# A hybrid decoder layer on one core: residual rows parked in device memory, six more raw weight buffers, and four seven-product pairs in nine of the gate/up blocks

## The chip, the core and the metric

The kernel runs on one core of a Trainium2 chip. The metric is the time of one execution on the device in microseconds. The kernel before takes 1085.96 us (median of three runs, 1085.82 to 1085.98). The profile is of one execution, recorded by the hardware.

## The reference

One decoder layer over 256 tokens with model width 2048 and a feed-forward width of 5632, all in float32:

```python
def reference(x, ln1_w, w_in, conv_w, ..., w_out, ln2_w, w_ffn_gate, w_ffn_up, w_ffn_down, final_norm_w):
    h = x
    for l in range(DEPTH):
        u = rmsnorm(h, ln1_w[l])
        proj = jnp.einsum('bsd,de->bse', u, w_in[l])
        lru_x, lru_g, q, k, v, ret_g = jnp.split(proj, SPLITS, axis=-1)
        ...
        y = jnp.concatenate([y_lru, y_ret], axis=-1)
        h = h + jnp.einsum('bse,ed->bsd', y, w_out[l])
        u = rmsnorm(h, ln2_w[l])
        ff = jax.nn.silu(jnp.einsum('bsd,df->bsf', u, w_ffn_gate[l])) * jnp.einsum('bsd,df->bsf', u, w_ffn_up[l])
        h = h + jnp.einsum('bsf,fd->bsd', ff, w_ffn_down[l])
    return rmsnorm(h, final_norm_w)
```

The change touches the output projection (`w_out`), the gate and up products of the feed-forward part, and what of the down product and the final norm hangs on them. `h`, the residual row, is needed at `w_out`, then for `u`, and then only at the down product.

## The kernel before

**A product.** TensorE (PE) multiplies in a reduced float32 format. Each float32 operand is split into a high part (a cast) and a low part (operand less high part), and `three` (L670 to L672) adds three matmuls: high by high, low weight by high left, high weight by low left. The left operands (tokens) are split once and kept. The weights, 235 MB, come past once: SyncE (SP) loads 512 KB at a time into a raw buffer (pool `raw`, six of 128x1024), ScalarE (ACT) casts it into `wh` (L112), VectorE (DVE) subtracts it into `wl` (L113); the pool `split` has four buffers each of `wh` and `wl`. `load` is called three loads ahead of the step that uses them (`AHEAD = 3`).

**Blocks.** From the output projection on, the program is a row of blocks: index 0 and 1 are `w_out`, 2 to 12 the eleven gate/up blocks (each 512 columns of gate and up), then the down product. A block has four accumulators (`c11`, `c12`, `c21`, `c22`: two token tiles by two halves of the columns) and eight quads of weights. A quad is 2x2 tiles b11, b12, b22, b21 in two loads, and it is multiplied in one of two ways:

- plain (`p`, `Block.plain`): eight products, 24 matmuls, two full splits.
- summed, a seven-product pair: DVE adds the quad's tiles into t1 to t4 (`Quad.add`, L648, four 128x512 adds), which are split too. Four products with b11, t1, t2 and t3 are added into the accumulators one block ahead (`s`, `Block.share`, 12 matmuls, loaded by `Shared`); three with b21, b22 and t4 follow in the block itself (`d`, `Block.direct`, 9 matmuls), for which `Direct` loads half of the weights again. That is seven products, 21 matmuls.

`SUMMED[i]` lists the summed quads of block i, `STEPS[i]` the order of its steps; its `s` steps belong to block i+1. After the last `s` of a block `share` combines the accumulators: two copies by ACT (L782, L785) and four operations on DVE (L783 to L787), and the next product that goes into `c12` has to wait for the second copy.

**Between blocks.** A gate/up block ends in `post`: ACT's Silu (L842) and DVE's multiplication (L844); then PE transposes (L833) and ACT copies the result into `ff` (L835). `Left` splits it and builds its sums for the down product (L551 to L554 on DVE). The output projection ends in `out_post`: DVE adds the residual rows `htok` (eight tiles of 128x512, pool `resid`, L585) and ACT squares them for the norm (L586).

**Order.** Each engine runs its instructions in the order that was fixed when the program was built: a scheduler takes the steps in the order of `program`, simulates the engines, and moves an instruction ahead of others where it could start earlier. An engine waits at its first instruction that is not ready. A cast into `wh` waits for the last matmul that reads the buffer's former content, a `wl` waits for the cast.

Of the kernel before, what the change touches and what calls it, by code (L numbers as in the profile page):

```python
# [31 lines left out]
SUMMED = ((), (4, 5), (2, 3)) + ((1, 2, 3), (0, 1, 2, 3)) * 4 + ((1, 2, 3), (1, 2, 3))  # L32
# [3 lines left out]
STEPS = ("pppspppspp", "ppspdpsdpp", "pdpsdpspspp") + ("pspsdpsdpsdp", "psdpsdpsddp") * 4 + ("psdpsdpsdpp", "psdpsdpsdpp")  # L36
# [8 lines left out]
def tile_hymba_layer(ctx: ExitStack, tc: tile.TileContext, A: dict, out: bass.AP):  # L45
# [5 lines left out]
    xpool = ctx.enter_context(tc.tile_pool(name="resid", bufs=8))  # L51
    rpool = ctx.enter_context(tc.tile_pool(name="raw", bufs=6))
    wpool = ctx.enter_context(tc.tile_pool(name="split", bufs=4))
    early = ctx.enter_context(ExitStack())
    epool = early.enter_context(tc.tile_pool(name="conv", bufs=2))
    tpool = early.enter_context(tc.tile_pool(name="tmp", bufs=6))
    late = []
# [12 lines left out]
    def res_tile(name, dt=F32):  # L70
        return xpool.tile([P, 512], dt, tag="xh", name=nm(name))
# [43 lines left out]
    class Unit:  # L115
# [8 lines left out]
        def load(self, j):  # L124
            raw = rpool.tile([P, 1024], F32, tag="raw", name=nm("raw"))
            h = wpool.tile([P, 1024], F32R, tag="wh", name=nm("wh"))
            l = wpool.tile([P, 1024], F32R, tag="wl", name=nm("wl"))
            n = 1024 // self.pieces
            for p in range(self.pieces):
                o = p * n  # L130
                nc.sync.dma_start(out=raw[:, o : o + n], in_=self.src[:, j * 1024 + o : j * 1024 + o + n])
                if self.before:
                    self.before(j * self.pieces + p)
            for p in range(self.pieces):
                o = p * n
                split(h[:, o : o + n], l[:, o : o + n], raw[:, o : o + n])
                if self.after:
                    self.after(j * self.pieces + p)
            self.h.append(h)
            self.l.append(l)  # L140
# [426 lines left out]

    def out_post(d):
# [13 lines left out]
        def post(c, ps):  # L582
            cb, t = 2 * d + int(c[2]) - 1, int(c[1]) - 1
            h = htok[cb, t]
            v.tensor_tensor(out=h, in0=ps, in1=h, op=ALU.add)  # L585
            act.activation(out=act_tile("junk"), in_=h, func=AF.Square, accum_out=sq2[:, t, cb : cb + 1])  # L586
            if t:
                turns.extend(lambda p=p: turn(p) for p in (2 * cb, 2 * cb + 1))
            if (cb, t) == (3, 1):
                v.tensor_reduce(out=v2, in_=sq2, axis=mybir.AxisListType.X, op=ALU.add)  # L590
                rsqrt_small(r2_tok, v2, 1.0 / D, 2)
# [12 lines left out]
    class Quad:  # L604
# [21 lines left out]
        def load(self, half):  # L626
            r = rpool.tile([P, 1024], F32, tag="raw", name=nm("raw"))
# [95 lines left out]
    class Shared(Quad):  # L723
# [4 lines left out]
        def load(self, half):  # L728
            r = rpool.tile([P, 1024], F32, tag="raw", name=nm("raw"))
# [17 lines left out]
    class Direct(Quad):  # L747
# [8 lines left out]
        def load(self, half):  # L756
            r = rpool.tile([P, 1024], F32, tag="raw", name=nm("raw"))
            nc.sync.dma_start(out=r, in_=self.src[:, 1024:2048])
            self.cut(("b22", "b21"), r)
            self.parts["t4"] = self.shared.parts["t4"]  # L760
# [97 lines left out]
    def load_fw():  # L858
        for c in range(4):
            fw[c] = late_tile("fw")  # L860
            nc.sync.dma_start(out=fw[c], in_=A["final_norm_w"][c * 512 : c * 512 + 512].partition_broadcast(P))
# [203 lines left out]
    def swap():  # L1065

        early.close()
        late.append(ctx.enter_context(tc.tile_pool(name="late", bufs=4)))

# [6 lines left out]
    for b, after in zip(blocks, blocks[1:] + [down]):  # L1076
        if b.index == 2:
            program.append(([], swap))
        b.put(after)
        if b.index == NB:  # L1080
            program.append(([], load_fw))
# [120 lines left out]
```

## Time and profile before

| | before |
|---|---|
| median of the runs | 1085.96 us |
| span of the profiled execution | 1084.4 us |
| gate/up blocks 3 to 12 end at | 476.3, 515.4, 560.4, 599.5, 644.5, 683.6, 728.6, 767.7, 811.0, 852.6 us |
| ACT CAST 128x1024 in the stage 432.3 to 852.6 us | 161 times, mean 1051 ns |
| DVE wl 128x1024 there | 160 times, mean 1218 ns |
| DVE adds L648 there | 136, mean 690 ns |
| mean DMA rate of the program | 220 GB/s |

The profiled execution has no time of its own but its span; the median lies 1.6 us above it. In the views, a row of the timeline gives start, length, engine, line, operation and the tiles out<-in; "x3" are instructions of one form run together, and a bracket at the end is the idle time before it and what ended it. Operations overlap a little at their ends, so start to start is the better measure of what an instruction occupies: a full split on DVE is written as 1218 ns and the next one starts 1.14 us after it. In the waits, "ACT wh L112 <- PE c L672" reads: ACT's cast into `wh` waited for a matmul.

### The profile page before, as it was taken

What the parts mean: (1) busy time and instruction counts of PE and PEld (TensorE: products, weight loads), DVE (VectorE), ACT (ScalarE), POOL (GpSimd) and SP (SyncE); (2) the same over time, 40 slices, a digit from 0 to 9 for tenths busy, and PEclk for the clock granted to TensorE, in tenths of its full rate; (3) what the DMA queues carried; (4) which work ended last, traced back from release to release, by engine and by line L of the source; (5) the groups of instructions that cost most, each with busy time, mean ns of one, the idle gap of its engine ahead of it and who ended that gap; (6) DMA issues with size and microseconds to landing.
All of it is one profiled execution on the core that took longest, in us unless ns stands there. A gap on an engine that the chain in (4) does not pass through costs nothing.

```text
span 1084.4 us, 14584 instructions
## 1 busy us (share of the span) xinstructions
PE 1074.2 (99%) x5101; PEld 899.5 (83%) x5101; DVE 953.5 (88%) x1371; ACT 660.9 (61%) x935; POOL 51.0 (5%) x61
## 2 busy tenths in 40 slices
PE   9999999999999999999999999999999999999997
PEld 7888888888888788888888888888888888888885
DVE  7789799988878889888998998999899899898986
ACT  7666644468746676565566566556556666655563
POOL 0612230000000000000000000000000000000001
PEclk9999999999999999999999999999999999999999
DMA  9964474444565567577677677686675756465652
GB/s 330 333 211 168 160 252 173 174 175 171 181 230 205 184 228 275 198 248 266 220 245 261 220 264 235 233 289 214 233 271 194 265 181 213 171 214 199 212 209 85
DMA packets 69274, 238.32 MB, mean 220 GB/s; under 512 B 7888, under 2 KB 8272, under 8 KB 69200
## 3 DMA queue, kind: packets, MB, share of 16 engines
q1 hardware_dynamic: 68400, 235.29, 62.7%
q0 software_dynamic: 512, 1.57, 0.4%
q8 instruction: 40, 0.66, 0.2%
q10 hardware_dynamic: 288, 0.52, 0.1%
q14 instruction: 34, 0.28, 0.1%
HBM read 235.26 MB, written 2.10 MB: 219 GB/s over the span
## 4 chain that ended last, share of the span: by engine, by line
PE 97%; DVE 1%; issue 1%; DMA 0%; ACT 0%; POOL 0%; SPq 0%; POOLq 0%; ACTq 0%
PE c L670 22%; PE c L672 22%; PE c L671 22%; PE fm L184 11%; PE fm L186 5%; PE tm L164 3%; PE tm L165 3%; PE tm L166 3%; PE p L672 1%; PE p L671 1%; PE p L670 1%; PE ft L833 1%; DMA raw<-in_w_v 0%; PE ht L576 0%; PE sc L482 0%
## 5 line engine op out<-in xcount | busy, mean ns | idle before, releaser
L112 ACT CAST wh<-raw 128x1024 fp32r<-128x1024 f32 (+1 forms) x490 | 460.9, 965 | 362.6 <-PE c L672 132.5
L113 DVE TENSOR_TENSOR wl<-raw,wh 128x1024 fp32r<-128x1024 f32 (+1 forms) x490 | 538.2, 1122 | 91.2 <-ACT wh L112 88.4
L671 PE MATMUL c<-wl,ah 128*128 128x512 f32 x850 | 331.0, 390 | 0.0
L672 PE MATMUL c<-wh,al 128*128 128x512 f32 x850 | 330.4, 389 | 0.0
L670 PE MATMUL c<-wh,ah 128*128 128x512 f32 x850 | 275.0, 391 | 0.2 <-ACT wh L112 0.2
L670 PEld LDWEIGHTS c<-wh,ah 128*128 128x128 f32 x850 | 159.4, 188 | 33.4 <-ACT wh L112 1.1
L672 PEld LDWEIGHTS c<-wh,al 128*128 128x128 f32 x850 | 159.6, 188 | 33.0
L671 PEld LDWEIGHTS c<-wl,ah 128*128 128x128 f32 x850 | 159.6, 188 | 32.7
L184 PE MATMUL fm<-u,wh 128*128 128x512 f32 x512 | 161.3, 396 | 0.0
L186 PEld LDWEIGHTS fm<-u,wl 128*128 128x128 f32 x512 | 96.0, 188 | 22.5
L186 PE MATMUL fm<-u,wl 128*128 128x256 f32 x512 | 101.1, 278 | 0.0
L184 PEld LDWEIGHTS fm<-u,wh 128*128 128x128 f32 x512 | 78.4, 189 | 0.3
L648 DVE TENSOR_TENSOR raw<-raw,raw 128x512 f32<-128x512 f32 x106 | 73.1, 690 | 2.8
L648 DVE TENSOR_TENSOR raw<-raw 128x512 f32<-128x512 f32 x106 | 72.7, 689 | 2.4
L671 PE MATMUL c<-wl,sh 128*128 128x512 f32 x176 | 68.5, 389 | 0.0
L672 PE MATMUL c<-wh,sl 128*128 128x512 f32 x176 | 68.0, 389 | 0.0
L670 PE MATMUL c<-wh,sh 128*128 128x512 f32 x176 | 60.4, 394 | 0.3 <-ACT sh L112 0.3
L165 PE MATMUL tm<-wl,u 128*128 128x512 f32 x128 | 48.8, 394 | 0.0
L166 PE MATMUL tm<-wh,u 128*128 128x512 f32 x128 | 48.7, 390 | 0.0
L164 PE MATMUL tm<-wh,u 128*128 128x512 f32 x128 | 47.3, 398 | 0.8 <-ACT u L288 0.8
L954 POOL TENSOR_TENSOR htok<-htok,fw 128x512 f32<-128x512 f32 x2 | 2.5, 1273 | 895.9 <-ACT junk L947 895.9
L670 PEld LDWEIGHTS c<-wh,sh 128*128 128x128 f32 x176 | 33.1, 188 | 7.3 <-ACT sh L112 0.7
(245 smaller groups left out, 1034.9 us busy)
## 6 DMA issues: line engine op xcount, KB each, us to landing
raw<-in_w_gu SPq DMA_DIRECT2D x212, 512.0 KB, 5.5
raw<-in_w_down SPq DMA_DIRECT2D x91, 512.0 KB, 4.3
raw<-in_w_out SPq DMA_DIRECT2D x34, 512.0 KB, 3.7
raw<-in_w_lx SPq DMA_DIRECT2D x16, 512.0 KB, 6.3
raw<-in_w_k SPq DMA_DIRECT2D x16, 512.0 KB, 3.5
raw<-in_w_q SPq DMA_DIRECT2D x16, 512.0 KB, 4.0
raw<-in_w_rg SPq DMA_DIRECT2D x16, 512.0 KB, 3.4
raw<-in_w_lg SPq DMA_DIRECT2D x16, 512.0 KB, 3.4
```

What stands on the lines that cost most here:

```text
L112: act.copy(out=dst_h, in_=src)
L113: v.tensor_tensor(out=dst_l, in0=src, in1=dst_h.bitcast(F32), op=ALU.subtract)
L164: pe.matmul(ps, ah, wh, start=first, stop=False)
L165: pe.matmul(ps, ah, wl, start=False, stop=False)
L166: pe.matmul(ps, al, wh, start=False, stop=last)
L184: pe.matmul(ps, wh, hl, start=n + i == 0, stop=False)
L186: pe.matmul(ps[:, :S], wl, hl[:, :S], start=False, stop=n + i == len(order) - 1)
L648: v.tensor_tensor(out=dst, in0=a, in1=b, op=ALU.add)
L670: pe.matmul(p, ah, bh, start=first, stop=False, skip_group_check=onto)
L671: pe.matmul(p, ah, bl, start=False, stop=False, skip_group_check=onto)
L672: pe.matmul(p, al, bh, start=False, stop=last, skip_group_check=onto)
L833: pe.transpose(pt[:, o : o + P], g[:, (2 * b + c) * P : (2 * b + c) * P + P], ident)
```

## The change

Three things change together.

- The residual rows are written to device memory as soon as they are made (eight stores issued by ACT in `out_post`), their pool and two others are closed ahead of block 3, and after the last block they are read back by eight DMAs on GpSimd's (POOL's) queue. The four loads of the final norm's weights go from SP to POOL and move behind block 12.
- In the space the pool `raw2` of six raw buffers is opened; loads go in turn to the old and the new pool from block 3 until ahead of block 12.
- Blocks 4 to 12 have four summed quads each; before, blocks 4, 6, 8 and 10 had four and 5, 7, 9, 11 and 12 had three. The step strings follow.

```diff
-SUMMED = ((), (4, 5), (2, 3)) + ((1, 2, 3), (0, 1, 2, 3)) * 4 + ((1, 2, 3), (1, 2, 3))
+SUMMED = ((), (4, 5), (2, 3), (1, 2, 3)) + ((0, 1, 2, 3),) * 9
 SUMMED_OUT, SUMMED_FFN = (4, 5), (0, 1, 2, 3)
 PLAIN = ((4, 5, 6, 7, 0, 1, 2, 3),) * 2 + (tuple(range(8)),) * 11
-STEPS = ("pppspppspp", "ppspdpsdpp", "pdpsdpspspp") + ("pspsdpsdpsdp", "psdpsdpsddp") * 4 + ("psdpsdpsdpp", "psdpsdpsdpp")
+STEPS = ("pppspppspp", "ppspdpsdpp", "pdpsdpspspp", "pspsdpsdpsdp") + ("psdpsdpsdpsd"[:-1]+"dp"[:0],)*0 + ("psdpsdsdpsdp",) * 8 + ("psdpsddpsdp",)
 EARLY_DOWN = (0, 1, 2)
...
     apool = ctx.enter_context(tc.tile_pool(name="acts", bufs=60))
-    xpool = ctx.enter_context(tc.tile_pool(name="resid", bufs=8))
     rpool = ctx.enter_context(tc.tile_pool(name="raw", bufs=6))
...
     early = ctx.enter_context(ExitStack())
+    xpool = early.enter_context(tc.tile_pool(name="resid", bufs=8))
     epool = early.enter_context(tc.tile_pool(name="conv", bufs=2))
     tpool = early.enter_context(tc.tile_pool(name="tmp", bufs=6))
-    late = []
+    late, resid, more, turn_of = [], [xpool], [], [0]
+    extra = ExitStack()
     pmm = ctx.enter_context(tc.tile_pool(name="pmm", bufs=4, space=PSUM))
...
     def res_tile(name, dt=F32):
-        return xpool.tile([P, 512], dt, tag="xh", name=nm(name))
+        return resid[0].tile([P, 512], dt, tag="xh", name=nm(name))
+    def raw_tile():
+        turn_of[0] += 1
+        pool_ = more[0] if more and turn_of[0] % 2 else rpool
+        return pool_.tile([P, 1024], F32, tag="raw", name=nm("raw"))
     def late_tile(name, dt=F32):
...
         def load(self, j):
-            raw = rpool.tile([P, 1024], F32, tag="raw", name=nm("raw"))
+            raw = raw_tile()
             h = wpool.tile([P, 1024], F32R, tag="wh", name=nm("wh"))
...
     turns = []
+    kept = nc.dram_tensor("kept_rows", (4, 2, P, 512), F32, kind="Internal").ap()
     def out_post(d):
...
             act.activation(out=act_tile("junk"), in_=h, func=AF.Square, accum_out=sq2[:, t, cb : cb + 1])
+            act.dma_start(out=kept[cb, t], in_=h)
             if t:
...
         def load(self, half):
-            r = rpool.tile([P, 1024], F32, tag="raw", name=nm("raw"))
+            r = raw_tile()
             nc.sync.dma_start(out=r, in_=self.src[:, half * 1024 : half * 1024 + 1024])
...
         def load(self, half):
-            r = rpool.tile([P, 1024], F32, tag="raw", name=nm("raw"))
+            r = raw_tile()
             nc.sync.dma_start(out=r, in_=self.src[:, half * 1024 : half * 1024 + 1024])
...
         def load(self, half):
-            r = rpool.tile([P, 1024], F32, tag="raw", name=nm("raw"))
+            r = raw_tile()
             nc.sync.dma_start(out=r, in_=self.src[:, 1024:2048])
...
             fw[c] = late_tile("fw")
-            nc.sync.dma_start(out=fw[c], in_=A["final_norm_w"][c * 512 : c * 512 + 512].partition_broadcast(P))
+            pool.dma_start(out=fw[c], in_=A["final_norm_w"][c * 512 : c * 512 + 512].partition_broadcast(P))
     ssq = cpool.tile([P, 2, 5], F32, name="ssq")
...
         early.close()
+        more.append(extra.enter_context(tc.tile_pool(name="raw2", bufs=6)))
+    def stop_more():
+        more.clear()
+    def swap_back():
+        extra.close()
         late.append(ctx.enter_context(tc.tile_pool(name="late", bufs=4)))
+        resid[0] = ctx.enter_context(tc.tile_pool(name="resid2", bufs=8))
+        for key in [(cb, t) for cb in range(4) for t in range(2)]:
+            htok[key] = res_tile("htok")
+            pool.dma_start(out=htok[key], in_=kept[key])
+        load_fw()
     blocks = [Block(d, lambda i, d=d: A["w_out"][8 * d + i], y, out_post(d), STEPS[d], SUMMED[d]) for d in range(2)]
...
     for b, after in zip(blocks, blocks[1:] + [down]):
-        if b.index == 2:
+        if b.index == 3:
             program.append(([], swap))
+        if b.index == NB + 1:
+            program.append(([], stop_more))
         b.put(after)
-        if b.index == NB:
-            program.append(([], load_fw))
+    program.append(([], swap_back))
     for d in range(2):
```

The line numbers of the changed kernel are six to nine higher (L113 is L119, L648 is L657, L670 to L672 are L679 to L681, L785 is L794). Counted over the whole program, PE has 15 matmuls fewer, DVE 35 instructions more (20 adds and 15 half splits), ACT 15 casts and 8 DMA issues more, SP one issue more (five weight loads more, four loads of the norm's weights fewer), POOL 12 DMAs more.

First place, DVE in a gate/up block. Before, between one shared step and the next there is a plain quad. The rows begin with the t1/t3 split of a shared quad (`wl_1184`); `wl_1189` is the split of a direct step, `wl_1181` and `t4l_1186` take t2 and t4, `wl_1192` and `wl_1195` are the two halves of a plain quad, `wl_1198` takes b11 of the next shared quad and `wl_1201` its t1/t3:

```order
L113 TENSOR_TENSOR wl_1184_5712<-raw_1179_5688,wh_1183_5711 128x1024
L113 TENSOR_TENSOR wl_1189_5722<-raw_1187_5719,wh_1188_5721 128x1024
L113 TENSOR_TENSOR wl_1181_5691<-raw_1182_5703,wh_1180_5690 128x512
L113 TENSOR_TENSOR t4l_1186_5716<-raw_1182_5703,t4h_1185_5715 128x512
L113 TENSOR_TENSOR wl_1192_5752<-raw_1190_5749,wh_1191_5751 128x1024
L113 TENSOR_TENSOR wl_1195_5758<-raw_1193_5755,wh_1194_5757 128x1024
L113 TENSOR_TENSOR wl_1198_5776<-raw_1196_5773,wh_1197_5775 128x512
L648 TENSOR_TENSOR raw_1196_5773<-raw_1196_5773 128x512
L648 TENSOR_TENSOR raw_1196_5773<-raw_1196_5773,raw_1199_5788 128x512
L648 TENSOR_TENSOR raw_1199_5788<-raw_1196_5773,raw_1199_5788 128x512
L648 TENSOR_TENSOR raw_1199_5788<-raw_1199_5788 128x512
L113 TENSOR_TENSOR wl_1201_5797<-raw_1196_5773,wh_1200_5796 128x1024
```

After the change, in a block with the string "psdpsdsdpsdp": `wl_1189` is t1/t3 of the second shared quad, `wl_1194` the direct step's, `wl_1186` and `t4l_1191` t2 and t4, `wl_1197` b11 and `wl_1200` t1/t3 of the third:

```order
L119 TENSOR_TENSOR wl_1189_5734<-raw_1184_5710,wh_1188_5733 128x1024
L119 TENSOR_TENSOR wl_1194_5744<-raw_1192_5741,wh_1193_5743 128x1024
L119 TENSOR_TENSOR wl_1186_5713<-raw_1187_5725,wh_1185_5712 128x512
L119 TENSOR_TENSOR t4l_1191_5738<-raw_1187_5725,t4h_1190_5737 128x512
L119 TENSOR_TENSOR wl_1197_5774<-raw_1195_5771,wh_1196_5773 128x512
L657 TENSOR_TENSOR raw_1195_5771<-raw_1195_5771 128x512
L657 TENSOR_TENSOR raw_1195_5771<-raw_1195_5771,raw_1198_5777 128x512
L657 TENSOR_TENSOR raw_1198_5777<-raw_1195_5771,raw_1198_5777 128x512
L657 TENSOR_TENSOR raw_1198_5777<-raw_1198_5777 128x512
L119 TENSOR_TENSOR wl_1200_5786<-raw_1195_5771,wh_1199_5785 128x1024
```

The two full splits of the plain quad are gone from between the two shared quads. On PE sixty matmuls lie in each of the blocks 4 to 11 between the last one that reads the buffer into which the plain half ahead of these rows is cast, and the first one that reads `wl_1200` or its counterpart.

Second place, PE at the end of block 12, where `c12` of the down product is combined. Before, the last shared product into `c12_1650` stands 37 rows above the last row here, with most of two plain quads between; these are the last of them and c12's next product:

```order
L671 MATMUL c12_1565_7489<-wl_1703_8097,ah_845_4126 128x512
L672 MATMUL c12_1565_7489<-wh_1702_8096,al_846_4127 128x512
L671 MATMUL c22_1563_7481<-wl_1703_8097,ah_845_4126 128x512
L672 MATMUL c22_1563_7481<-wh_1702_8096,al_846_4127 128x512
L670 MATMUL c11_1647_7858<-wh_1707_8106,ah_1705_8102 128x512
L671 MATMUL c11_1647_7858<-wl_1708_8107,ah_1705_8102 128x512
L672 MATMUL c11_1647_7858<-wh_1707_8106,al_1706_8103 128x512
L670 MATMUL c11_1647_7858<-wh_1710_8136,ah_1705_8102 128x512
L670 MATMUL c12_1650_7870<-wh_1707_8106,ah_1705_8102 128x512
```

After, the last shared product into `c12_1674` is the first row and c12's next product the last:

```order
L681 MATMUL c12_1674_7957<-wh_1706_8089,sl_1705_8086 128x512
L680 MATMUL c11_1585_7559<-wl_1721_8157,ah_845_4129 128x512
L681 MATMUL c11_1585_7559<-wh_1720_8156,al_846_4130 128x512
L680 MATMUL c21_1587_7567<-wl_1721_8157,ah_845_4129 128x512
L681 MATMUL c21_1587_7567<-wh_1720_8156,al_846_4130 128x512
L680 MATMUL c12_1588_7571<-wl_1721_8157,ah_845_4129 128x512
L681 MATMUL c12_1588_7571<-wh_1720_8156,al_846_4130 128x512
L680 MATMUL c22_1586_7563<-wl_1721_8157,ah_845_4129 128x512
L681 MATMUL c22_1586_7563<-wh_1720_8156,al_846_4130 128x512
L679 MATMUL c11_1671_7945<-wh_1728_8187,ah_1726_8183 128x512
L680 MATMUL c11_1671_7945<-wl_1729_8188,ah_1726_8183 128x512
L679 MATMUL c12_1674_7957<-wh_1728_8187,ah_1726_8183 128x512
```

Ten matmuls lie between now. The copy that the last of these rows waits for stands on ACT in this place (`wh_1757` goes into the buffer of `wh_1720`, `q_1724` is copied into `c12_1674`):

```order
L118 CAST wh_1728_8187<-raw_1725_8181 128x1024
L118 CAST wh_1731_8202<-raw_1730_8200 128x1024
L118 CAST wh_1736_8212<-raw_1733_8206 128x1024
L118 CAST ah_1726_8183<-ff_1011_4922 128x512
L118 CAST wh_1757_8293<-raw_1756_8291 128x1024
L118 CAST ah_1734_8208<-ff_1090_5288 128x512
L794 COPY c12_1674_7957<-q_1724_8174 128x512
```

Before, the copy into `c12_1650` stands behind two such casts on ACT, and 36 matmuls lie between on PE.

## The prediction

> **What bounds the kernel now.** I read the page first, then the stretch that the change works on, then single instructions.
>
> ```profile
> PE 1074.2 (99%) x5101; PEld 899.5 (83%) x5101; DVE 953.5 (88%) x1371; ACT 660.9 (61%) x935; POOL 51.0 (5%) x61
> PE 97%; DVE 1%; issue 1%; DMA 0%; ACT 0%; POOL 0%; SPq 0%; POOLq 0%; ACTq 0%
> 560.40:599.50 39.10, 39.10 (x178) 32.42 (x177) 34.97 (x44) 23.47 (x31) 0.00 (x0) 1.00 0.72 247
> 599.50:644.50 45.00, 45.00 (x205) 37.28 (x203) 41.15 (x52) 26.41 (x36) 0.00 (x0) 1.00 0.71 241
> ```
>
> The first two lines are busy time and the chain that ended last: PE is 97% of it. The next two are windows over two gate/up blocks, one with four summed quads and one with three (length; busy time and count of PE, PEld, DVE, ACT, POOL; granted clock; DMA share; GB/s). PE has no gap there and runs at full clock, so removed matmuls are removed time, while DVE is already busy for (34.97 + 41.15) / 84.1 = 90%. A summed quad buys PE time with DVE time. The question is whether the last tenth of DVE can be spent without PE waiting.
>
> ```profile
> ACT wh L112 <- DVE raw L648: 37.8, 14, 3.0
> ACT wh L112 <- PE c L672: 29.6, 26, 2.2
> DVE wl L113 <- ACT wh L112: 14.2, 12, 1.8
> ACT wh L112 <- DMA raw<-in_w_gu: 0.2, 1, 0.2
> ```
>
> These are the waits of 560.4 to 728.6 us, four blocks (total, times, longest). ACT waits for a matmul to give back one of the four wh buffers (26 times), DVE then waits for ACT's cast (12 times). A late weight load shows once, for 0.2 us. Raw buffers are what the change adds; split buffers are what the engines wait for.
>
> **PE's saving.**
>
> ```profile
> 614.81 0.39 PE L670 MATMUL c<-t4h,ah 128*128 128x512 f32 x1
> 615.09 4.09 DVE L113 TENSOR_TENSOR wl<-raw,wh 128x1024 fp32r<-128x1024 f32 x4
> 617.30 0.39 PE L671 MATMUL c<-wl,sh 128*128 128x512 f32 x1
> L648 DVE TENSOR_TENSOR raw<-raw,raw 128x512 f32<-128x512 f32 x106 | 73.1, 690 | 2.8
> L113 DVE TENSOR_TENSOR wl<-raw,wh 128x512 fp32r<-128x512 f32 x67 | 45.8, 683 | 7.9 <-ACT wh L112 7.8
> L112 ACT CAST wh<-raw 128x512 fp32r<-128x512 f32 x67 | 41.4, 618 | 26.8 <-PE c L672 26.3
> ```
>
> The first three lines are timeline rows (start, length, engine, line), the others groups with their count, busy time and mean ns, L648 of the whole program and L113 and L112 of the gate/up stage. From 614.81 to 617.30 PE starts eleven more matmuls, so one takes 2.49 / 11 = 0.2264 us. Five more summed quads are five products of three matmuls fewer: 15 x 0.2264 = **-3.40 us**. Their price lies on the others: per quad four adds of 0.690 and three half splits of 0.683 on DVE, 4.81 us, 24.0 in all; three half casts of 0.618 on ACT, 9.3 in all; one more 512 KB load on SP. As a sum that would still fit under PE (a block of four summed quads has about 41 us of DVE in 41.7 of PE), but with almost nothing left to recover a delay.
>
> **The new sequence s, d, s.** In the eight blocks with the new step string the third shared step follows the second with one direct step between. In the old strings a plain quad stood between any two shared steps. The price is read from a chain that the old kernel's timeline already shows:
>
> ```profile
> 571.29 0.39 PE L672 MATMUL c<-wh,sl 128*128 128x512 f32 x1
> 571.51 0.61 PE L670 MATMUL c<-wh,ah 128*128 128x512 f32 x2
> ...
> 571.71 1.76 ACT L112 CAST wh<-raw 128x1024 fp32r<-128x1024 f32 x2 [1.39 <-PE c L672]
> 576.19 2.52 ACT L112 CAST wh<-raw 128x1024 fp32r<-128x1024 f32 x3 [2.72 <-DVE raw L648]
> ...
> 572.80 1.83 DVE L113 TENSOR_TENSOR wl<-raw,wh 128x1024 fp32r<-128x1024 f32 x2 [1.83 <-ACT wh L112]
> 574.66 0.69 DVE L648 TENSOR_TENSOR raw<-raw 128x512 f32<-128x512 f32 x1
> 575.38 1.42 DVE L648 TENSOR_TENSOR raw<-raw,raw 128x512 f32<-128x512 f32 x2
> 576.84 0.69 DVE L648 TENSOR_TENSOR raw<-raw 128x512 f32<-128x512 f32 x1
> 577.45 2.95 DVE L113 TENSOR_TENSOR wl<-raw,wh 128x1024 fp32r<-128x1024 f32 x3
> 580.32 0.68 DVE L113 TENSOR_TENSOR t4l<-raw,t4h 128x512 fp32r<-128x512 f32 x1
> 580.92 1.22 DVE L113 TENSOR_TENSOR wl<-raw,wh 128x1024 fp32r<-128x1024 f32 x1
> ```
>
> At 571.29 PE starts the last matmul that reads a direct step's wh buffer. ACT's cast into it starts 0.42 us later, DVE's subtract at 572.80, and DVE then does without a pause: a plain half and b11 (1.86), four adds (2.79), three splits up to t2 (2.87), t4 (0.60), until 580.92: 9.63 us from the last matmul. The changed order has exactly these rows after the first direct step, but what follows is b11 of the third summed quad (0.72, which is 1.86 less 1.14 for the full split), its adds (2.79) and its t1/t3 split (1.22). That makes 9.63 + 0.72 + 2.79 + 1.22 = 14.36 us until PE can use t1's low part. In the changed PE order sixty matmuls lie between these two points in each of blocks 4 to 11: 60 x 0.2264 = 13.58. PE waits 0.78 us. A plain quad between would give 24 x 0.2264 = 5.43 of PE for two DVE splits of 1.14, 3.2 in hand, which is why the old strings don't wait; even so the t1/t3 split that began at 615.09 is used at 617.30, one microsecond after it is done. The wait comes again in each block, because DVE idles again at the next buffer that it waits for: 8 x 0.78 = **+6.2 us**.
>
> **Into block 12.** Block 12's summed quads make way for those of the down product, whose left operands DVE also has to build.
>
> ```profile
> 820.30 0.68 DVE L113 TENSOR_TENSOR al<-ff,ah 128x512 fp32r<-128x512 f32 x1
> 820.90 0.28 DVE L551 TENSOR_TENSOR s<-ff 128x128 f32<-128x128 f32 x1
> 821.10 0.28 DVE L553 TENSOR_TENSOR s<-ff 128x128 f32<-128x128 f32 x1
> ```
>
> By the order, from the last shared product of block 11 there are on DVE two full splits, q, al, four sums, b11, two combinations and two adds, then on ACT a cast, two gates and the cast that PE waits for. With 1.51 to the first split, 2 x 1.14, 0.6 for q and for al, 0.2 for a sum, 0.72, 0.6 for a combination, 0.7 for an add, then 0.95 and 1.05 for the casts and 0.6 for a gate, I get 11.7 to 12.3 us (some of it may overlap) against 48 matmuls, 10.87: 0.8 to 1.4, between 0 and 2 if an overlap is misjudged. I take **+1.0**, nearer to the lower end.
>
> **Out of block 12.** Here the last shared product is late: the old order has two plain quads behind it, the new one the end of one.
>
> ```profile
> 847.10 1.05 ACT L112 CAST wh<-raw 128x1024 fp32r<-128x1024 f32 x1 [1.04 <-DMA raw<-in_w_down]
> 848.05 0.61 ACT L112 CAST ah<-ff 128x512 fp32r<-128x512 f32 x1
> 848.57 1.05 ACT L112 CAST wh<-raw 128x1024 fp32r<-128x1024 f32 x1
> 849.52 0.62 ACT L112 CAST ah<-ff 128x512 fp32r<-128x512 f32 x1
> 850.04 0.58 ACT L785 COPY c<-q 128x512 f32<-128x512 f32 x1
> ```
>
> ACT must copy q into c12 (850.04 before the change) ahead of c12's next product. In the new order that copy stands behind a cast into the buffer of wh_1720, whose last reader is the third matmul ahead of that product. So PE waits 0.42 (release) + 0.95 (cast, 847.10 to 848.05) + 0.52 (ah, 848.05 to 848.57) + 0.58 (copy) less 3 x 0.2264 = **+1.8 us**. Bounds: 0 if ACT had the copy first, 2.5 if no matmul covers it.
>
> **The residual rows.**
>
> ```profile
> ACT wh L112 <- PE c L672: 1.2, 1, 1.2
> ACT wh L112 <- DMA raw<-in_w_gu: 1.2, 1, 1.2
> L986 ACTq DMA_DIRECT2D out<-htok x2: 380/421/462, 1079.3 to 1079.7; - x2
> decay<-in_decay POOLq DMA_DIRECT2D x8, 192.0 KB, 6.2
> 811.00:852.60 41.60, 41.60 (x189) 34.28 (x188) 39.70 (x57) 28.00 (x39) 0.00 (x0) 1.00 0.63 222
> ```
>
> The eight stores are issued by ACT between its squares and casts; one such issue took 0.42 us (the only ACT-issued DMA of the old trace). Four of them fall around 385 to 390 us, where ACT in the 25 us from 380 on waits a few times only (the first two lines): 1.7 us of issue against waits of 1.2. The bounds are 0 and 1.7; I take **+0.2**, since these casts feed PE over leads of more than a microsecond. What hides the rest is ACT's idle time; without it the whole 3.4 us of eight issues would be paid. The way back (eight rows of 256 KB and four of the final norm's weights) moves to POOL's queue, idle in this stretch, and takes four issues off SP. It is 3 MB while the block's weights use 0.63 of the DMA time at 222 GB/s (last line), so about 130 GB/s are free and it needs some 24 us; the rows are wanted long after that. I take 0, bounds 0 and +2: ACT's wait of 1.04 us for a weight at 847.10 shows that the loads there have no lead to give away. Six more raw buffers I also count at 0: they could remove the 0.2 us above.
>
> **The sum.** -3.40 + 6.2 + 1.0 + 1.8 + 0.2 = +5.8. The profiled span is 1084.4, so the new one would be 1090.2; the median of the runs is 1085.96, 1.6 above the span, which puts the time at **1091.8 us**.
>
> **The rivals.**
>
> *The buffers come back earlier than I count (faster).* Which matmul gives a buffer back I read off the order, four buffers back on its tag. If the cast had a buffer that was free already, the chain would be 14.36 - 1.51 = 12.85, below 13.58. It decides at four matmuls (0.78 / 0.2264 = 3.4) in the s, d, s sequence and at eight on the way out of block 12. With every stall hidden this gives 1085.96 - 3.4 + 0.2 = 1082.8. For it: the saving on PE is certain. Against it: the waits name exactly this release, 26 times in four blocks. The Trainium skill, Perfetto Trace Analysis, section Optimization Strategy, says that the same gap coming back on the engine that should be saturated can mean too little SBUF for the next tile. By that rule the repeated 1.8 us of DVE would go with the larger pool and the time would be this rival's; the trace agrees that buffers are short, but the engine that should be saturated is PE and has no gap, and the short ones are wh and wl, which stay at four.
>
> *Only the steady sequence fits.* If DVE and ACT gain the 0.78 us somewhere in each block but the ends stay: 1085.96 - 3.4 + 0.2 + 2.8 = 1085.6, no change. The margin is five per cent of a chain of 14 us.
>
> *Only the steady sequence waits.* Blocks 4 to 11 as forecast, the way into and out of block 12 hidden: 1085.96 - 3.4 + 6.2 + 0.2 = 1089.0.
>
> *The way back collides.* The 3 MB slow down the weights of block 12 just when the six extra raw buffers are given up, and ACT's wait of 1.04 comes several times: +2 to +4, 1094 to 1096. The Trainium skill, DMA: Bandwidth & Descriptors, section Issuing engines are not separate DMA queues, says that transfers of all engines share the same 16 DMA engines and interleave, so POOL's queue would save only issue time; no run here shows it yet.
>
> *The extra buffers do nothing.* That is part of my forecast: the change would then have bought its five quads with DVE time alone, and a kernel with the same order and six raw buffers would take the same time.
>
> **How the numbers follow.** Forecast 0.56 (1089.5 to 1093.5); only the steady sequence waits 0.12 (1089.0); collision 0.11 (1094 to 1096); only the ends wait 0.12 (1085.6); all hidden 0.09 (1082.8). Of a measurement, 0.2% or 2.2 us is about what can be told from no change, so faster is below 1083.8 and slower above 1088.1: faster 0.09, same 0.12, slower 0.79. The range leaves out the case of all hidden and most of the collision, and takes in the bounds of the ends: 1085.2 to 1095.0.
>
> **What would show it.** PE's busy time some 3.4 us lower, but idle time in front of L680 (c<-wl,sh) with DVE's wl as its releaser, about 0.8 us once per block in blocks 4 to 11, eight or so in all; one gap near 812 us behind ACT's cast or gate; one of nearly 2 us near 850 behind the copy into c12. DVE rises to about 977 us, ACT to about 670. Waits for raw loads stay near zero in blocks 4 to 10. The prediction is wrong if PE shows no gaps in those blocks, if DVE's splits ahead of the third shared step start without waiting for ACT, or if the gaps are named by a DMA.

## The result and the profile after

The changed kernel takes 1093.33 us (median of four runs) against 1085.97 for the kernel before: 7.4 us slower, ratio 1.0070 (95% interval 1.0056 to 1.0084). The prediction was 1091.8, range 1085.2 to 1095.0. The profiled execution has a span of 1092.8 us, 8.4 over the one of before; that execution took 1094.61, 1.3 over the median, and one microsecond of it went at the very start, where PE's first products at 6 to 10 us started 0.43 us apart for longer than in the profile of before.

The busy times of the changed kernel, the window of one gate/up block (length; busy time and count of PE, PEld, DVE, ACT, POOL; granted clock; DMA share; GB/s), and the two largest of PE's waits:

```profile
PE 1078.1 (99%) x5086; PEld 896.0 (82%) x5086; DVE 975.4 (89%) x1406; ACT 668.5 (61%) x950; POOL 57.9 (5%) x73
562.00:605.00 43.00, 42.65 (x191) 34.56 (x190) 40.68 (x51) 25.78 (x34) 0.00 (x0) 1.00 0.76 250
PE c L679 <- ACT wh L118: 2.6, 10, 0.7
PE c L679 <- ACT c L794: 1.3, 1, 1.3
```

PE is "99% busy" before and after, and its busy time has even risen by 4 us although 15 matmuls are gone. That number hides the loss: a matmul stands 390 ns in the record while the next one starts 227 ns after it, so a pause is covered by the tail of the matmul ahead of it, and the matmul behind it is recorded as longer (500 ns). The loss is seen in the starts. These are PE's starts in one of the blocks with the new string, from the last reader of the first direct step's `wh` buffer (573.85) to the first reader of the third shared quad's `wl` (588.35):

```profile
573.62 0.39 PE L680 MATMUL c<-wl,sh 128*128 128x512 f32 x1
573.85 0.39 PE L681 MATMUL c<-wh,sl 128*128 128x512 f32 x1
...
586.09 0.39 PE L680 MATMUL c<-wl,ah 128*128 128x512 f32 x1
586.31 0.39 PE L681 MATMUL c<-wh,al 128*128 128x512 f32 x1
586.84 0.73 PE L679 MATMUL c<-wh,sh 128*128 128x512 f32 x2
587.79 0.50 PE L679 MATMUL c<-wh,ah 128*128 128x512 f32 x1 [0.21 <-ACT wh L118]
588.12 0.40 PE L679 MATMUL c<-wh,sh 128*128 128x512 f32 x1
588.35 0.40 PE L680 MATMUL c<-wl,sh 128*128 128x512 f32 x1
```

From 586.31 to 588.35 five starts should take 5 x 0.227 = 1.13 us and take 2.04: a loss of **0.9 us**, in two pauses. The wait that the view names is 0.21. The same sum, start to start less 0.227, over all eight blocks with the new string gives 0.90 to 0.91 each, 7.2 us together, at the same place of each block. From 573.85 to 588.35 PE has sixty starts (59 matmuls lie between the two), which should take 13.6 us and take 14.50. DVE and ACT in the same stretch:

```profile
575.36 1.82 DVE L119 TENSOR_TENSOR wl<-raw,wh 128x1024 fp32r<-128x1024 f32 x2 [1.49 <-ACT wh L118]
577.22 0.69 DVE L657 TENSOR_TENSOR raw<-raw 128x512 f32<-128x512 f32 x1
577.95 1.42 DVE L657 TENSOR_TENSOR raw<-raw,raw 128x512 f32<-128x512 f32 x2
579.40 0.69 DVE L657 TENSOR_TENSOR raw<-raw 128x512 f32<-128x512 f32 x1
580.01 2.96 DVE L119 TENSOR_TENSOR wl<-raw,wh 128x1024 fp32r<-128x1024 f32 x3
582.88 0.68 DVE L119 TENSOR_TENSOR t4l<-raw,t4h 128x512 fp32r<-128x512 f32 x1
583.49 0.68 DVE L119 TENSOR_TENSOR wl<-raw,wh 128x512 fp32r<-128x512 f32 x1
584.20 0.69 DVE L657 TENSOR_TENSOR raw<-raw 128x512 f32<-128x512 f32 x1
584.93 1.42 DVE L657 TENSOR_TENSOR raw<-raw,raw 128x512 f32<-128x512 f32 x2
586.38 0.69 DVE L657 TENSOR_TENSOR raw<-raw 128x512 f32<-128x512 f32 x1
586.99 3.49 DVE L119 TENSOR_TENSOR wl<-raw,wh 128x1024 fp32r<-128x1024 f32 x3
...
574.27 1.76 ACT L118 CAST wh<-raw 128x1024 fp32r<-128x1024 f32 x2 [1.00 <-PE c L681]
585.73 3.47 ACT L118 CAST wh<-raw 128x1024 fp32r<-128x1024 f32 x4 [3.44 <-DVE raw L657]
```

573.85, then 0.42 to the cast, DVE at 575.36 and no pause until the t1/t3 split ends (586.99 + 1.22 = 588.21): 14.36 us, as predicted to the hundredth. DVE idles 1.49 us at the head of the chain, so it isn't short of time; it is kept from starting.

The end of block 12, PE and then ACT:

```profile
859.77 0.39 PE L681 MATMUL c<-wh,al 128*128 128x512 f32 x1
860.27 0.50 PE L679 MATMUL c<-wh,ah 128*128 128x512 f32 x1
860.61 0.40 PE L680 MATMUL c<-wl,ah 128*128 128x512 f32 x1
862.30 0.50 PE L679 MATMUL c<-wh,ah 128*128 128x512 f32 x1 [1.29 <-ACT c L794]
...
860.19 1.05 ACT L118 CAST wh<-raw 128x1024 fp32r<-128x1024 f32 x1
861.14 0.61 ACT L118 CAST ah<-ff 128x512 fp32r<-128x512 f32 x1
861.66 0.58 ACT L794 COPY c<-q 128x512 f32<-128x512 f32 x1
```

859.77 to 862.30 is 2.53 us for three starts (0.68); with 0.11 more behind the last pause, 1.96 us are lost. ACT's cast, `ah` and the copy run back to back from the buffer's release. A third place, on the way into block 12, loses 0.94 us behind the matmul that starts at 825.95; PE waits there for a cast that stands behind the two gates on ACT:

```profile
827.01 0.50 PE L679 MATMUL c<-wh,ah 128*128 128x512 f32 x1 [0.66 <-ACT wh L118]
...
824.77 1.25 ACT L851 ACTIVATE gated<-c,r_tok 128x512 f32<-128x512 f32 x2
825.91 2.51 ACT L118 CAST wh<-raw 128x1024 fp32r<-128x1024 f32 x3
```

Sum by starts: 7.2 + 1.96 + 0.94 = 10.1 lost, 3.4 gained.

### The profile page after: what moved, and what is told of

Read it like the earlier page. It is cut to its first block, busy times and chain, and to the rows that moved or that the text cites. A ratio compares the mean times of both kernels' runs of the same rounds, so it can differ in the third digit from the quotient of the medians.

```text
span 1092.8 us, 14647 instructions
## 1 busy us (share of the span) xinstructions
PE 1078.1 (99%) x5086; PEld 896.0 (82%) x5086; DVE 975.4 (89%) x1406; ACT 668.5 (61%) x950; POOL 57.9 (5%) x73
## 5 line engine op out<-in xcount | busy, mean ns | idle before, releaser
L119 DVE TENSOR_TENSOR wl<-raw,wh 128x1024 fp32r<-128x1024 f32 (+1 forms) x500 | 542.3, 1111 | 70.8 <-ACT wh L118 68.4
L680 PE MATMUL c<-wl,ah 128*128 128x512 f32 x820 | 319.4, 390 | 0.0
L681 PE MATMUL c<-wh,al 128*128 128x512 f32 x820 | 318.1, 390 | 0.0
L679 PE MATMUL c<-wh,ah 128*128 128x512 f32 x820 | 270.1, 393 | 4.0 <-ACT wh L118 2.6
L679 PEld LDWEIGHTS c<-wh,ah 128*128 128x128 f32 x820 | 153.9, 188 | 40.7 <-ACT wh L118 7.5
L681 PEld LDWEIGHTS c<-wh,al 128*128 128x128 f32 x820 | 154.0, 188 | 32.0
L680 PEld LDWEIGHTS c<-wl,ah 128*128 128x128 f32 x820 | 154.0, 188 | 31.5
L657 DVE TENSOR_TENSOR raw<-raw,raw 128x512 f32<-128x512 f32 x116 | 80.1, 691 | 3.7 <-DMA raw<-in_w_down 0.6
L657 DVE TENSOR_TENSOR raw<-raw 128x512 f32<-128x512 f32 x116 | 79.6, 689 | 2.7
L680 PE MATMUL c<-wl,sh 128*128 128x512 f32 x196 | 76.5, 390 | 0.0
L681 PE MATMUL c<-wh,sl 128*128 128x512 f32 x196 | 75.8, 389 | 0.0
L679 PE MATMUL c<-wh,sh 128*128 128x512 f32 x196 | 69.2, 399 | 1.4 <-ACT sh L118 0.3
L679 PEld LDWEIGHTS c<-wh,sh 128*128 128x128 f32 x196 | 36.2, 188 | 11.5 <-ACT wh L118 4.5
L680 PEld LDWEIGHTS c<-wl,sh 128*128 128x128 f32 x196 | 36.8, 188 | 8.8 <-DVE wl L119 1.4
```

The source lines that it names most:

```text
L119: v.tensor_tensor(out=dst_l, in0=src, in1=dst_h.bitcast(F32), op=ALU.subtract)
L657: v.tensor_tensor(out=dst, in0=a, in1=b, op=ALU.add)
L679: pe.matmul(p, ah, bh, start=first, stop=False, skip_group_check=onto)
L680: pe.matmul(p, ah, bl, start=False, stop=False, skip_group_check=onto)
L681: pe.matmul(p, al, bh, start=False, stop=last, skip_group_check=onto)
```

## The experiments

Theory A is that of the prediction: the loss is made by the distance, in PE work, between the release of a split buffer and the use of what has to go through it. Each ratio is to runs of the kernel before on the same chip.

**Each half of the change alone.** First the changed kernel with the old tables (`STEPS` goes with `SUMMED`), then the kernel before with the new tables:

```diff
-SUMMED = ((), (4, 5), (2, 3), (1, 2, 3)) + ((0, 1, 2, 3),) * 9
+SUMMED = ((), (4, 5), (2, 3)) + ((1, 2, 3), (0, 1, 2, 3)) * 4 + ((1, 2, 3), (1, 2, 3))
...
```

> The changed kernel with the summed quads and step strings of before: rows parked, six more raw buffers, read back by POOL, nothing else. Theory A (all of the loss is in the new step order): the eight store issues cost 0.2 us, the buffers and the way back nothing, so 1086.0 to 1086.6 us, no gap in PE over 0.1 us between 480 and 800 us. Rival C (the stores, the way back or the alternation of two raw pools cost the time): 1089 us or more, with PE or ACT waiting for a DMA near 830 to 860 us or near 385 us.

```diff
-SUMMED = ((), (4, 5), (2, 3)) + ((1, 2, 3), (0, 1, 2, 3)) * 4 + ((1, 2, 3), (1, 2, 3))
+SUMMED = ((), (4, 5), (2, 3), (1, 2, 3)) + ((0, 1, 2, 3),) * 9
...
```

> The kernel before with the summed quads and step strings of after: rows stay in SBUF, six raw buffers, no way back. Theory A (a cast waits for a wh buffer, not for a raw buffer or a load): the same gaps of about 0.9 us in blocks 4 to 11, 1092.5 to 1093.5 us. Rival C (the residual rows' traffic costs it): about 1086 us. Rival D (the six raw buffers do help the new order): 1095 us or more, with raw loads named in the waits.

Measured: 1087.11 us, ratio 1.0007 (0.9998 to 1.0017), for the rows and buffers alone; 1093.76, ratio 1.0067 (1.0052 to 1.0082), for the tables alone, with the same pauses in the same places. Both times lie a little above what was expected (by 0.5 and 0.3 us); the kernel before took 1086.23 beside them. The whole loss comes with the tables. The parked rows and the six raw buffers together cost less than the measurement can tell. No run has the one without the other, so a small cost of the rows and a small gain of the buffers could cancel; but ACT waits for late loads only once between 440 and 870 us of the changed kernel, for 1.4 us, which leaves the buffers little to gain. Rivals C and D fall.

**Is it the distance, or DVE's total work?** Two kernels give PE four matmuls more in each of the eight blocks, by adding one product five times and not once, either behind the release of the buffer or ahead of it. The instruction orders of DVE, ACT and SP are the same rows as in the changed kernel. The edit of the first; the second has `m == 0`:

```diff
         def direct(self, m, quad):
             for c, a, b in DIRECT:
-                three(self.ps[c], self.lefts[self.summed[m]][a], quad.parts[b], False, False, True)
+                three(self.ps[c], self.lefts[self.summed[m]][a], quad.parts[b], False, False, True); [pe.matmul(self.ps[c], self.lefts[self.summed[m]][a][1], quad.parts[b][0], start=False, stop=False, skip_group_check=True) for _ in range(4 * (c == 'c12' and m == 1 and 4 <= self.index <= 11))]
```

> The changed kernel with one matmul (the low left by high weight product into c12) of the second direct step of blocks 4 to 11 issued five times, not once: 4 x 8 = 32 matmuls more, 7.3 us of PE work, on a result that is thereby not the reference's. They stand between the release of the first direct step's wh buffer and the first use of the third shared quad; the orders of the other engines are the same rows. Theory A (PE waits there 0.9 us for a chain that began at the release): the four matmuls fill the gap, 1093 to 1094 us, gaps of 0.1 us or less at that place. Rival F (the gap is added by each block's total DVE work or by the pace of loads, so that added PE work just delays the whole): 1098 to 1101 us.

> The same four matmuls more, of the first direct step: they repeat the very matmul that is the last to read the wh buffer the chain waits for, so the release and all that follows come 0.91 us later. The orders of the other engines are the same rows. Theory A (only the distance from the release to the use counts): nothing is hidden, the gaps stay at 0.9 us and the time grows by 32 x 0.2264 = 7.2 us to 1100 to 1101 us. Rival B (DVE's total work is the bound and PE has 0.9 us a block to spare anywhere): 1093 to 1094 us, as in the run beside it.

Behind the release: 1094.22 us, ratio 1.0068 (1.0053 to 1.0083), as the changed kernel, though PE has 32 x 0.227 = 7.3 us more to do. Ahead of it: 1102.16, ratio 1.0140 (1.0123 to 1.0157). Both lie above the expected ranges, by 0.2 and 1.2 us. The blocks themselves fit: from the transposes at 484.6 us to those at 827.6 the changed kernel takes 343.0 us, the first kernel 343.7 for the same stretch and the second 350.2. The place in the first kernel, its added matmuls in the second line:

```profile
584.95 0.39 PE L681 MATMUL c<-wh,sl 128*128 128x512 f32 x1
585.18 1.07 PE L800 MATMUL c<-wh,sl 128*128 128x512 f32 x4
586.09 0.39 PE L680 MATMUL c<-wl,sh 128*128 128x512 f32 x1
```

They sit where PE would have paused, and the pauses are gone but for 0.11 us. In the second kernel the added matmuls are themselves the last readers; ACT's cast waits for them, and the pauses behind it are as long as ever:

```profile
576.94 1.07 PE L800 MATMUL c<-wh,sl 128*128 128x512 f32 x4
...
578.04 1.05 ACT L118 CAST wh<-raw 128x1024 fp32r<-128x1024 f32 x1 [1.90 <-PE c L800]
...
591.55 0.50 PE L679 MATMUL c<-wh,ah 128*128 128x512 f32 x1 [0.21 <-ACT wh L118]
```

In these eight blocks the same 32 matmuls cost 0.7 us in one place and 7.2 in the other. That settles the mechanism of the pauses at s, d, s: theory A is shown, rivals B and F fall.

**Can another order avoid it?** One string changed, two direct steps in place of one between the shared steps that stand close:

```diff
-("psdpsdsdpsdp",) * 8
+("psddspsdpsdp",) * 8
```

> The changed kernel with one step string altered: blocks 4 to 11 as psddspsdpsdp, so that two direct steps, not one, stand between the two shared steps that have no plain quad between them. Products, loads and splits are the same in number. Theory A (order: too little PE work between two shared steps): a direct step more gives 9 x 0.2264 = 2.04 us of PE against 1.14 of DVE, 0.90 in hand against a gap of 0.89, so the gaps in blocks 4 to 11 shrink to 0.1 or nothing and the time to 1086.0 to 1087.0 us. Rival B (DVE at 97% of PE's time can't keep up in any order of four and four): 1092 us or more.

Measured: 1097.89 us, ratio 1.0106 (1.0091 to 1.0121). A miss: slower still, with as many products, loads and splits. The time is one that rival B had named, so DVE at that place decides:

```profile
616.07 1.22 DVE L119 TENSOR_TENSOR wl<-raw,wh 128x1024 fp32r<-128x1024 f32 x1
618.56 0.69 DVE L119 TENSOR_TENSOR wl<-raw,wh 128x512 fp32r<-128x512 f32 x1 [1.28 <-ACT wh L118]
```

Four buffers now hold the first shared quad's two tiles and the two direct steps', so the second shared quad's b11 waits for the first direct step to be used up (its last matmul starts at 617.48, the cast 0.42 us later) before its adds may even start. I had counted PE and DVE work between the shared steps, and not which buffer is free. It is the buffers again, not DVE, which idles 1.28 us.

Then the spacing made regular across the ends of the blocks, with and without parked rows:

```diff
-("psdpsdsdpsdp",) * 8 + ("psdpsddpsdp",)
+("dspdspdspdsp",) * 8 + ("dspdspdspdp",)
...
-    run = lambda m=m, quad=quad: self.direct(m, quad)
+    run = lambda m=m, quad=quad, k=k: self.direct(m, quad, k == 0)
...
+            while first and turns:
+                turns.pop(0)()
```

> The changed kernel with blocks 4 to 11 as dspdspdspdsp and block 12 as dspdspdspdp: the same steps, but a direct step and a plain quad stand between any two shared steps, across the ends of blocks too. The transposes that stood in the first plain quad follow the first direct step. Theory A (only the spacing of the shared steps makes PE wait): PE has 33 x 0.2264 = 7.5 us between two shared steps where the chain of splits and adds after a released buffer needs about 2.3 us less than that allows, so no gaps in blocks 4 to 11, and the last shared product of block 12 has a plain quad more behind it, which takes the 1.9 us there away: 1083 to 1085.5 us, faster than both kernels. Rival B (DVE at 97% can't keep up in any order): 1090 us or more. Rival E (a shared step so early in a block waits for the accumulators of the block two before, whose last product has only just ended): a gap of 1 us or more at the start of each block, 1091 us or more.

> The kernel before (rows in SBUF, six raw buffers) with the changed kernel's summed quads and the same regular step strings as in the run beside this one. Theory A: six raw buffers are enough, the time is that of the run beside it within 0.5 us. Rival D (with DVE nearly full the extra raw buffers do take up delays of loads): slower than it by 1 us or more, with raw loads named in the waits.

Measured: 1112.70 us, ratio 1.0238 (1.0223 to 1.0253), and 1112.47 without parked rows. A miss again. Inside the blocks PE doesn't pause at all, as A had it, but some 2.8 us are lost at each start of a block. The windows of one such start and of the rest of that block, and PE's largest wait between 440 and 870 us (total, times, longest):

```profile
519.00:528.00 9.00, 7.32 (x29) 4.85 (x28) 8.99 (x13) 5.83 (x8) 0.00 (x0) 1.00 0.61 228
528.00:564.00 36.00, 36.00 (x165) 29.79 (x164) 31.95 (x40) 20.28 (x26) 0.00 (x0) 1.00 0.71 244
PE c L680 <- DVE wl L119: 12.3, 10, 1.4
```

DVE is full for nine microseconds: the four combinations of the accumulators and the four adds of the next block's first shared quad now fall together, ahead of the split that PE needs. Rival E's place was right; its reason was right in small part only, since PE's waits for the accumulators' last combination come to 1.5 us. Rival B's number was met, but not its reason: DVE idles four of the other 36 us, so it isn't its total that is too much but what falls together. The pair of runs shows once more that the parked rows and the six raw buffers together change nothing.

**The freed space for split buffers.** The parked rows' space was given to more pairs of `wh` and `wl`. The edit for seven pairs; the others have one pair and four raw buffers, or two pairs and two raw buffers, in the place of three pairs:

```diff
-        more.append(extra.enter_context(tc.tile_pool(name="raw2", bufs=6)))
+        more.append(extra.enter_context(tc.tile_pool(name="split2", bufs=3)))
...
+    def split_tiles():
+        turn_of[0] += 1
+        pool_ = more[0] if more and turn_of[0] % 7 in (1, 3, 5) else wpool
+        return [pool_.tile([P, 1024], F32R, tag=g, name=nm(g)) for g in ("wh", "wl")]
...
-            h, l = (wpool.tile([P, 1024], F32R, tag=g, name=nm(g)) for g in ("wh", "wl"))
+            h, l = split_tiles()
```

> The changed kernel with the parked rows' space given to three more pairs of wh and wl buffers (seven each in blocks 3 to 11) in place of six raw buffers; order of steps as in the change. Theory A (the chain starts with a cast that waits for the last reader of a wh buffer): without that wait the chain has 1.5 us less, which is more than the gap, so the gaps in blocks 4 to 11 go: 1085.5 to 1087 us, with the two gaps around block 12 left. Rival B (DVE has no time left): PE still waits once a block, now for a split or an add, 1091 us or more.

> As the run with seven pairs of split buffers, but the parked rows' space is shared: one pair of wh and wl more (five) and four raw buffers more (ten) in blocks 3 to 11. That run lost the gap of the s, d, s sequence in its first two blocks and then waited for raw loads (23 waits, 48 us on ACT). Theory A (split buffers hold up s, d, s, and with seven of them six raw buffers became too few): no gap at s, d, s, no waits for loads, 1086 to 1088 us. Rival B (with more split buffers the engines' orders change and that, not the raw buffers, cost 16 us): 1093 us or more, gaps at other places in each block.

> The same with two pairs of split buffers more (six) and two raw buffers more (eight). Theory A: between the run with seven and six (1109.8) and the run with five and ten, nearer to the latter if loads are the limit: 1086 to 1092 us, with some waits for raw loads. Rival B: 1093 to 1110 us with as few waits for loads as in the run with five and ten.

Measured: seven pairs and six raw buffers 1109.76 us, ratio 1.0214 (1.0196 to 1.0232); five and ten 1110.29, 1.0214 (1.0195 to 1.0233); six and eight 1099.47, 1.0116 (1.0101 to 1.0132). All miss theory A's times. The short pauses at s, d, s are gone or rare, as A had it, but longer ones (up to 3.3 us) come around the end of some blocks, while the accumulators are combined. With ten raw buffers late loads aren't their cause, since no wait for one shows between 440 and 870 us; with six, ACT waits 44 us for loads in that stretch, and the shares of loads and order aren't told apart. With more buffers the scheduler fixed other orders on DVE and ACT. In the run with five pairs DVE comes to the split that PE needs (611.07) only behind another split and a combination:

```profile
608.87 0.50 PE L685 MATMUL c<-wh,ah 128*128 128x512 f32 x1
612.35 0.50 PE L686 MATMUL c<-wl,ah 128*128 128x512 f32 x1 [2.97 <-DVE wl L125]
...
609.34 1.22 DVE L125 TENSOR_TENSOR wl<-raw,wh 128x1024 fp32r<-128x1024 f32 x1
610.48 0.68 DVE L799 TENSOR_TENSOR q<-p,c 128x512 f32<-128x512 f32 x1
611.07 2.95 DVE L125 TENSOR_TENSOR wl<-raw,wh 128x1024 fp32r<-128x1024 f32 x3
```

Whether one more pair would pay in the order of the change was not tried: every change of the buffers changes the order too.

**Block 12.** First the changed kernel with the last two direct steps of block 12 moved behind its last shared step, then the kernel before with one summed quad more, by its own alternation:

```diff
-("psdpsddpsdp",)
+("psdpsdpsddp",)
```

> The changed kernel with block 12 as psdpsdpsddp in place of psdpsddpsdp: the same steps, the second pair of direct steps behind the last shared step. 28 matmuls then lie between the last shared product into c12 and c12's next product, ten before. Theory A: the gap of 1.9 us at the end of block 12 goes, the others stay: 1091 to 1092 us. Rival G (the gap is made by the weights of the down product or the 3 MB that are read back): it stays or moves, 1093 us.

```diff
-SUMMED = ((), (4, 5), (2, 3)) + ((1, 2, 3), (0, 1, 2, 3)) * 4 + ((1, 2, 3), (1, 2, 3))
+SUMMED = ((), (4, 5), (2, 3)) + ((1, 2, 3), (0, 1, 2, 3)) * 5
...
-STEPS = ("pppspppspp", "ppspdpsdpp", "pdpsdpspspp") + ("pspsdpsdpsdp", "psdpsdpsddp") * 4 + ("psdpsdpsdpp", "psdpsdpsdpp")
+STEPS = ("pppspppspp", "ppspdpsdpp", "pdpsdpspspp") + ("pspsdpsdpsdp", "psdpsdpsddp") * 5
```

> The kernel before with its own alternation of blocks of three and four summed quads continued to block 12 (three in block 11, four in block 12; strings pspsdpsdpsdp and psdpsdpsddp): one summed quad more than before, no s, d, s, rows kept, six raw buffers. Theory A: three matmuls fewer, 0.7 us, and no new gap: 1085.0 to 1085.6 us, the best of all, though by less than a measurement can tell. Rival B: any summed quad more costs DVE time and the time rises, 1087 us or more.

Measured: 1093.26 us, ratio 1.0059 (1.0044 to 1.0074), and 1088.50, ratio 1.0017 (1.0008 to 1.0027). Both miss. In the first the copy into c12 no longer holds PE, but 1.3 of the 1.96 us stay:

```profile
858.90 0.50 PE L679 MATMUL c<-wh,ah 128*128 128x512 f32 x1
859.24 0.40 PE L680 MATMUL c<-wl,ah 128*128 128x512 f32 x1
860.25 0.50 PE L681 MATMUL c<-wh,al 128*128 128x512 f32 x1 [0.61 <-DVE al L119]
```

Behind the copy stand the next late things: PE stops at 858.90 for `ah`, the high part of the down product's left operand, and at 860.25 for `al`, its low part. ACT makes `ah` only behind a cast that waited for a load of the down product's weights. The same cast waits in the second kernel, which stops at the same two places; ACT in the first and then in the second:

```profile
857.28 1.05 ACT L118 CAST wh<-raw 128x1024 fp32r<-128x1024 f32 x1 [1.02 <-DMA raw<-in_w_down]
858.24 1.13 ACT L118 CAST ah<-ff 128x512 fp32r<-128x512 f32 x2
...
853.67 1.05 ACT L112 CAST wh<-raw 128x1024 fp32r<-128x1024 f32 x1 [1.15 <-DMA raw<-in_w_down]
854.63 1.13 ACT L112 CAST ah<-ff 128x512 fp32r<-128x512 f32 x2
```

So rival G stands for what stays, as far as it names the weights; how much of it they make was not tested. The rows' way back is not needed for it, since the second kernel has none. In the changed kernel itself ACT waits for no load there. In the second kernel, which has no s, d, s at all, the two pauses around block 12 come with its fourth summed quad: 0.89 us at 820 and 1.8 at 854. They take 2.7 and the quad saves 0.7, about the 2.1 us measured. In both strings of block 12 that were run here a fourth summed quad costs PE time on both sides of that block, though what PE waits for on the way out is not the same. No version that was run is faster than the kernel before.

## Why the prediction was right

- **PE's saving, -3.40 us:** the 15 matmuls are gone, and the busy time of PE's weight loads shows it (899.5 to 896.0). PE's own busy time doesn't, as told above; the sign that I had named for this step was wrong.
- **s, d, s, +6.2 us:** right in mechanism, place and number of places; measured 7.2. The chain was 14.36 us as read from the old trace, and the sixty starts of PE were right. The term was too small by 0.13 us a block because I let the wait end with the `wl` split, while PE uses it 14.50 us after the release. PE stops a few matmuls earlier, at two `wh` casts (586.84 and 587.79 above), and after each pause the next matmul comes 0.11 us late. The releaser is thus ACT, not DVE as I had written. The split, done at 588.21, would have held PE nearly as long (without the pauses PE would have been there at 587.45), so which of the two it was makes little difference to the size.
- **Into block 12, +1.0:** measured 0.94, behind the gates and the cast that I had counted; that it fell so close, in a sum of 0.8 to 1.4, is luck. **Out of it, +1.8:** measured 1.96. Size and chain right, but the copy was not the only thing late there: in the order that takes its delay away 1.3 us stay.
- **Residual rows, +0.2:** the rows and buffers alone gave a ratio of 1.0007, whose interval holds it. The eight stores took ACT 0.33 us each to issue (median), not the 0.42 of the two in the old trace. POOL's read-back landed in 4.9 us (median), and weights were not late for it, although the DMA share rose to 0.85 in that stretch; the collision didn't come.
- **Extra raw buffers, 0:** nothing seen in three pairs of runs (old tables, new tables, regular order), each time together with the parked rows.
- **The sum:** -3.4 + 7.2 + 0.9 + 2.0 = 6.7 of the 7.4 us. Where the other 0.7 goes is open; it is less than what the kernel before itself drifts between sets of runs (1085.97 to 1086.90).

The Trainium skill's sentence on repeated gaps (Perfetto Trace Analysis, section Optimization Strategy) was to the point in that buffers are what is short; the six that were added are of a kind that ACT hardly ever waited for.

## What to carry to other kernels

When two engines feed a third through a small ring of buffers, the price of a tighter order can be read before it is built: follow the chain from the instruction that releases a buffer to the use of what goes through it, and compare it with the work of the waiting engine between these two instructions in the new order. Spare time on the feeding engines (10% here) says little, since they stand idle at the head of such a chain; and more buffers of a kind that no engine waits for change nothing. Look at starts, not at busy time: an engine that is "99% busy" lost 10 us.

## What was not expected of the hardware

After longer pauses PE runs at half pace for a while. In the run with five pairs of split buffers, the windows around a pause of 3.25 us:

```profile
608.00:613.00 5.00, 1.93 (x8) 1.05 (x7) 4.87 (x6) 4.43 (x7) 0.00 (x0) 1.00 0.48 189
613.00:618.00 5.00, 5.00 (x17) 3.96 (x16) 4.14 (x7) 0.54 (x1) 0.00 (x0) 0.66 0.62 213
```

The granted clock is 0.66 of full speed in the mean of the window after it, and for three microseconds a matmul takes 0.43 us, not 0.227. It also came after two pauses of 1.65 and 1.81 us with one matmul between, and after one of 2.05 with one of 0.25 just ahead. It never came in the changed kernel or the regular order, where no single pause is over 1.6 us; but in the run with seven pairs two pauses of 1.26 and 1.51 us, a third of a microsecond apart, were enough, while in the regular order 1.27 and 1.45 us, 1.5 us apart, were not. So the length of a single pause doesn't decide it. The Trainium skill (TensorE: Matmul & The Clock Gate, section HAM oscillation — how this bites in real kernels) speaks of idle gaps above some 3.4 us; here some 2.3 us of pauses were enough once. This made the three runs with more split buffers slower than their pauses alone.
